# One queue of side units for VectorE through the first mixer, and a tile of their own for the new keys and values

## The chip, the cores and the metric

The kernel runs on one core of a Trainium2 chip. The metric is the time of one execution on the device in microseconds (us), lower is better. Of several runs the median is given. A separate execution is taken by the hardware profiler; its page and its trace are what is read here. TensorE is called PE in the profile, VectorE DVE, ScalarE ACT, GpSimd POOL, SyncE SP; PEld is TensorE's weight load. The program has some 47,500 instructions and is one straight line without loops on the device.

## The reference, cut to what matters

The kernel computes one inference step of a small diffusion backbone with two layers, for 128 context tokens and 128 latent tokens side by side (256 columns in the kernel). D_MODEL is 2048, everything is 32-bit floating point.

```python
for l in range(DEPTH):                                  # DEPTH = 2
    mod = jax.nn.silu(cond) @ w_ada[l] + b_ada[l]       # cond: 2 vectors, w_ada[l]: 2048 x 12288
    sh1, sc1, gt1, sh2, sc2, gt2 = jnp.split(mod[:, None, :], 6, axis=-1)
    h = rmsnorm(x, g_norm_mix[l]) * (1 + sc1) + sh1
    m = mixer_ab(h, ...) if l % 2 == 0 else mixer_c(h, ...)
    x = x + gt1 * m
    h = rmsnorm(x, g_norm_ffn[l]) * (1 + sc2) + sh2
    x = x + gt2 * conv_ffn(h, ...)

def mixer_ab(h, ...):                                   # the first mixer
    proj = h @ w_in                                     # query latent, key/value latent, rope key, qb, kb, vb
    q_lat, ckv, k_rope = ...
    kb = rmsnorm(kb, g_kn); vb = ...                    # 2 heads of new keys and values
    qa = rmsnorm(q_lat, g_q) @ w_q_up                   # 8 heads
    kv = concatenate([cached ckv, rmsnorm(ckv, g_kv)]) @ w_kv_up
    out_a = softmax_attention(qa, keys of kv and k_rope, values of kv)
    out_b = softmax_attention(qb, concatenate([cached k, kb]), concatenate([cached v, vb]))
    return concatenate([out_a, out_b]) @ w_out, (ckv, k_rope, kb, vb)
```

The new ckv, k_rope, kb and vb of the context tokens are outputs too, so the kernel stores them from the tiles in which they are made.

## The kernel before

**Large products.** Every weight matrix is read once from HBM in tiles of 1 MB (`raw`). ScalarE makes the high half of each (`wh`, L222), VectorE the low half (`wl`, L223), and TensorE multiplies three times for each block of 128 x 128: high by high, high by low, low by high (L317, L318, L321). A product of 16 blocks is 48 matmuls into one of three PSUM banks `acc`.

**The first mixer** (`mixer_ab`) runs in stages. The input projection is done in quarters of the 2048 input features, each with 23 products; the sums of the quarters are kept in `pr` (15 chunks: 6 of the query latent, 4 of the key/value latent, 1 rope key, 2 keys `kb`, 2 values `vb`) and `qb` (8 chunks). VectorE adds each product to them (L821). In the last quarter (`q == 3`) `finish` starts chains of small steps on the finished chunks: `latents` normalises the latents and stores them (L762), `keys` normalises and rotates the keys and stores them (L787), `values` transposes the values. Then come the heads: 12 products of the queries and 16 of keys and values, with two attention heads in flight between them. A query product is copied out of PSUM by ScalarE into `qn` (L903). Last is the output projection, 16 products, each followed by `residual` (L633) and a sum of squares on GpSimd (L178).

**SBUF.** The tiles of the mixer are in the pool `ab`; `ckc` and `pr` are in the pool `abp`, which is closed at the end of the input projection. The tiles of the heads (`qn`, `qr`, `p`, `kn`, `vt`, ...) are in `abh`, which is laid over the place of `abp`. A tile there waits for the last reader of the old tile that it lies over, a store to HBM among them. `pr` is one tile for this purpose.

**adaLN beside the products.** The product of the two condition vectors with w_ada (100 MB for each layer) is cut in units of 512 outputs, 48 for both layers, and mixed into the stages. There are three ways: TensorE sums rows (`sum_rows`, L445, with tiles `araw` of 1 MB, two buffers); VectorE reduces features (in the feed-forward parts); and in the first mixer a third one, the side units: 16 blocks of 256 KB for each unit (`block`, three buffers, L472), and two accumulations on VectorE for each block, one for each condition vector (`sum_block`: L456 for the first block, L459 for the others), then three small steps that reduce the two sums over partitions on TensorE, copy and transpose them. That is 16 + 3 = 19 steps for a unit. `sum_block` pins its instructions in the program's order.

**How much of it where.** After each product `pump` is called. It adds `side["rate"]` to a due count and does a step of the side units for each whole one, and the same with `RATE` for the rows. In the list of the 33 units that are summed by rows, numbers 16 to 19 are the side units: 16, 17 and 18 from the last quarter of the input projection on, with 0.6 steps a product, in the heads with 1.2, and what is left at the end of the heads is done there by `side_flush`; 19 in the output projection with 1.25. Each of the two groups has its own pair of sums `aacc` and its own blocks, in `ab` and in a pool `abo` that is laid over `ab`.

**The order on the engines** is not the program's: a scheduler gives each engine's instructions an order by its own model of the machine, except for pinned ones. Each engine then works strictly in that order, and waits at an instruction whose semaphores are not there yet. All transfers are issued by SP in one queue.

Of the kernel before, what the change touches and what calls it, by code (L numbers as in the profile page):

```python
# [17 lines left out]
P = 128  # L18
D = 2048
KD = D // P  # L20
T = 128
NT = 2 * T
# [25 lines left out]
    _AT[_name] = (_n, _w)  # L48
    _n += _w
NCONST = _n  # L50
RATE = {"in0": 0.35, "in": 0.5, "in3": 0.25, "heads": 0.75, "out0": 0.6, "c": 0.65, "outc": 0.65}
FRATE = {"up": 0.7, "down": 1.42}
PEW = {"heads": 1.0, "out0": 1.0, "c": 0.5}
QUIET = [4, 3, 3]
# [15 lines left out]
ROWS = [(0, j, q) for q in range(4) for j in (1, 0)]  # L70
# [10 lines left out]
FLIMIT = {"ab": 0, "ffn0": 12, "c": 12, "ffn1": 15}  # L81
SUMMED = [22, 24, 26, 28, 31]

BESIDE = ([16, 17, 18], [19])
SIDE = {"in3": 0.6, "heads": 1.2, "out0": 1.25}
INV = {2048: 0, 768: 1, 512: 2, 128: 3, 256: 4}


# [1 line left out]
def step_kernel(ctx: ExitStack, tc: tile.TileContext, A: dict):  # L90
    nc = tc.nc
    pe, dve, act, pool, sp = nc.tensor, nc.vector, nc.scalar, nc.gpsimd, nc.sync
# [20 lines left out]
    def T_(pl, shape, tag, dt=F32, bufs=None):  # L113
        kw = {} if bufs is None else {"bufs": bufs}
        return pl.tile(shape, dt, tag=tag, name=nm(tag), **kw)
# [109 lines left out]
    fine = [False]  # L225
# [100 lines left out]
    ada = {"i": 2, "t": 0, "due": 0.0, "pew": 1.0}  # L326
# [149 lines left out]
            side["then"] = ada_finish(*u, True, side["acc"])  # L476
            side["units"].pop(0)

    def side_start(name, units, pool_, acc):
        side.update(units=[ROWS[u] for u in units], pool=pool_, acc=acc, rate=SIDE[name], due=0.0)  # L480

    def side_pump():
        side["due"] += side["rate"]
        while side["due"] >= 1.0:
# [3 lines left out]
    def side_flush():  # L488
        while side["units"] or side["then"]:
            side_step()  # L490
# [99 lines left out]
    def modulated(st, l, which, W, fixed):  # L590


        ensure(l, 3 * which + 1)
        ensure(l, 3 * which)
        while later:
            later.pop(0)()
        if which and not l:
            ada["i"] += len(BESIDE[0]) + len(BESIDE[1])
        u = ROWS[ada["i"]]
        tile_ = lambda t: T_(wpool, [P, 4, 512], "araw", bufs=2)  # L600

        def load_tile(t):
            raw = tile_(t)
            sp.dma_start(out=raw, in_=A["w_ada"][u[0], u[1], u[2], t])
            return raw

        raws = [load_tile(0), load_tile(1)]
        hx = T_(keep, [P, KD, ROW], "hx", F32R)
        r = stat_rstd(st, D, att_bank)
        sum_rows(0, raws[0], bank())  # L610
        rb = spread(diagonal(r, (0, 1)), bank=att_bank)
        sum_rows(1, raws[1])
        raws += [load_tile(2), load_tile(3)]
        modulate(hx, rb, l, which, range(KD), fixed)
        ada["i"] += 1
        rest = ada_finish(*u, False)

        def last_rows():
            sum_rows(3, raws[3])
            rest[0]()  # L620

        def turn():
            rest[1](tc.keep_in_program_order)

        ps = first_three(W, lambda k: hx[:, k, :NT], lambda k: hx[:, k, NT:2 * NT],
                         AS_MADE if fixed else IN_TURN, lambda: sum_rows(2, raws[2]), fixed)
        W.ahead(lambda i: i)
        return hx, ps, [last_rows, turn]

    def residual(ps, l, which, c, st=None):  # L630
        for g in range(2):
            s = slice(g * T, (g + 1) * T)
            dve.scalar_tensor_tensor(out=x[:, c, s], in0=ps[:, s],  # L633
                                     scalar=mod[:, l, 3 * which + 2, c, g:g + 1],
                                     in1=x[:, c, s], op0=ALU.mult, op1=ALU.add)
        if st is not None:
            stat_add(st, x[:, c], KD)
# [62 lines left out]
        split(hx[:, c, :NT], hx[:, c, NT:2 * NT], o[:, :NT])  # L700


    def mixer_ab(hx, rb0, st):
        l = 0
        with tc.tile_pool(name="ab", bufs=1) as ab:
            with tc.tile_pool(name="abp", bufs=1) as pj:
                T_(ab, [P, SHIFT // 4], "pad")
# [15 lines left out]
                qb = T_(ab, [P, 8, NT], "qb")  # L723
                rsb = T_(ab, [P, 8, 2], "rsb")
                rsm = T_(ab, [P, 2], "rsmla")
                pr = T_(pj, [P, 15, NT], "proj")
                ck, kb, vb = pr[:, 6:10], pr[:, 11:13], pr[:, 13:15]
                sq, sk = stat_init(), stat_init()

                def queries(c):  # L730
# [82 lines left out]
                def part(W, k0, n, first, rate, between=None, **kw):  # L813

                    for c in range(23):
                        ps = gemm(W.chunk(), lambda k: hx[:, k0 + k, :NT], lambda k: hx[:, k0 + k, NT:2 * NT])
                        to = pr[:, c] if c < 15 else qb[:, c - 15]
                        if first:
                            act.copy(to, ps)
                        else:  # L820
                            dve.tensor_tensor(out=to, in0=to, in1=ps, op=ALU.add)  # L821
                        if between:
                            between(c)
                        pump(rate, **kw)
# [22 lines left out]
                for q in range(1, 4):  # L847
                    ensure(0, 1, [q])
                    ensure(0, 0, [q])
                    pinned[0] = q == 3  # L850
                    if q == 3:
                        caches()
                        acc = T_(ab, [P, 2, 512], "aacc")
                        side_start("in3", BESIDE[0], ab, [acc[:, 0], acc[:, 1]])
                    modulate(hx, rb0, 0, 0, range(4 * q, 4 * q + 4))
                    if q < 3:
                        part(W, 4 * q, 4, False, RATE["in"], until=2 * (q + 2))
                    else:
                        part(W, 4 * q, 4, False, RATE["in3"], finish)

            with tc.tile_pool(name="abh", bufs=1) as hp:
# [70 lines left out]

                    start(values_and_head(h, vt, qn[h], qr, kn))
                flush()
                side_flush()

        ensure(l, 2)
        ada["pew"] = PEW["out0"]
        W = Weights(A["w_out_ab"], KD, 1)
        oh, ol = (lambda k: o[:, k, :NT]), (lambda k: o[:, k, NT:2 * NT])  # L940
        with tc.tile_pool(name="abo", bufs=1) as abo:
            acc = T_(abo, [P, 2, 512], "aacc")
            side_start("out0", BESIDE[1], abo, [acc[:, 0], acc[:, 1]])
            for c in range(KD):
                fine[0] = c >= KD - QUIET[1]
                residual(gemm(W.chunk(), oh, ol, first=8), l, 0, c, st)
                pump(RATE["out0"] if c < KD - QUIET[1] else 0)
            side_flush()


    def mixer_c(cp, hx, W, ready, todo, st):
# [184 lines left out]
    with banks("pab") as ppool["ada"]:  # L1136
        ppool["att"] = ppool["ada"]
        for c in range(0, KD, 4):
            sp.dma_start(out=x[:, c:c + 4], in_=A["xT"][:, c:c + 4])
        first = {1: load_half(1, 0, "araw"), 0: load_half(0, 0, "raw")}  # L1140
        half_unit(1, 0, first[1], tc.keep_in_program_order)
        st = stat_init()
        for c in range(KD):
            stat_add(st, x[:, c], KD, dve)
        rb0 = norm_scale(st)
        half_unit(0, 0, first[0], tc.keep_in_program_order)
        hx = T_(keep, [P, KD, ROW], "hx", F32R)
        st = stat_init()
        mixer_ab(hx, rb0, st)
        W = Weights(A["w_up"][0], KD, 1)  # L1150
        hx, ready, todo = modulated(st, 0, 1, W, False)
    stage[0] = "ffn0"
    st = stat_init()
# [160 lines left out]
```

## Time and profile before

| | us |
|---|---|
| median of 3 runs | 2374.95 |
| lowest and highest run | 2369.23, 2376.01 |
| profiled execution | 2372.41 |
| its span, first to last instruction | 2370.6 |
| TensorE busy in the span | 2312.9 |
| VectorE busy | 1857.6 |
| ScalarE busy | 1165.7 |
| GpSimd busy | 179.7 |

The profiled execution is 1.8 us longer than its span, which is what lies around the instructions. The mean granted clock of TensorE is 0.993. The first mixer lies between about 27 and 460 us of the span: its last quarter of the input projection ends near 213 us, the heads near 363 us, and the output projection near 456 us. In the rows of waits the form is: engine, tile and line that waited, what it waited for, us in total, times, longest. In the rows of groups it is: line, engine, operation, tiles and shapes, count, then busy us, mean ns of one, and idle time of the engine just before with what ended it. In the rows of a timeline it is: start, length, engine, line, operation, tiles, count, and in brackets the idle time before. A busy TensorE is not TensorE at its peak, since matmuls are pipelined: neighbouring matmuls start about 0.11 us apart and are listed with 0.28 us each.

### The profile page before, as it was taken

The numbers are of one execution on the slowest core, as the hardware profiler recorded it, in microseconds if no ns is written. First come the engines' busy times: TensorE is split into PE (matmuls) and PEld (weight loads), VectorE is DVE, ScalarE is ACT, GpSimd is POOL, SyncE is SP. The second block draws the span as 40 slices with busy tenths as digits, with TensorE's granted clock in tenths as the row PEclk, the third lists the DMA queues.
The fourth block names the chain that finished last, engine by engine and source line by source line (L and its number), as shares of the span: only waits on it lengthen the run. The fifth ranks groups of instructions, "written<-read, shape, count | busy, mean of one in ns | idle before, by whom it ended". The sixth has DMA issues, their size and how long they took to land. (4 is left out here: it accounts for less than half of the span.)

```text
span 2370.6 us, 47563 instructions
## 1 busy us (share of the span) xinstructions
PE 2312.9 (98%) x19624; PEld 2189.4 (92%) x19624; DVE 1857.6 (78%) x2886; ACT 1165.7 (49%) x1857; POOL 179.7 (8%) x210
## 2 busy tenths in 40 slices
PE   6999999999999999999999999999999999999997
PEld 4688878899999999999989999998999999999997
DVE  3569868879999999999879887888899755666654
ACT  4345544465554355554465444446555434555543
POOL 0002211200000000001220100112000000000011
PEclk9999999999999999999999999999999999999999
DMA  9988777867777877777766787777677555555553
GB/s 370 365 306 300 291 292 263 325 223 257 267 267 275 308 265 259 263 259 274 284 232 243 286 292 278 280 292 273 246 260 259 208 196 196 194 193 191 192 194 123
DMA packets 99608, 612.95 MB, mean 259 GB/s; under 512 B 10752, under 2 KB 18624, under 8 KB 29632
## 3 DMA queue, kind: packets, MB, share of 16 engines
q1 hardware_dynamic: 99392, 609.92, 70.4%
q8 instruction: 154, 2.52, 0.4%
q14 instruction: 62, 0.51, 0.1%
HBM read 605.12 MB, written 4.75 MB: 257 GB/s over the span
## 5 line engine op out<-in xcount | busy, mean ns | idle before, releaser
L222 ACT CAST wh<-raw 128x1024 fp32r<-128x1024 f32 (+1 forms) x822 | 795.6, 979 | 914.8 <-PE acc L318 745.1
L223 DVE TENSOR_TENSOR wl<-raw,wh 128x1024 fp32r<-128x1024 f32 (+1 forms) x822 | 922.0, 1138 | 312.8 <-ACT wh L222 305.9
L317 PE MATMUL acc<-hx,wh 128*128 128x256 f32 x4064 | 1131.6, 279 | 4.1 <-ACT hx L583 3.0
L321 PE MATMUL acc<-hx,wl 128*128 128x256 f32 x4064 | 1125.5, 278 | 2.5 <-DVE wl L223 2.2
L318 PE MATMUL acc<-hx,wh 128*128 128x256 f32 x4064 | 1127.0, 278 | 0.0
L317 PEld LDWEIGHTS acc<-hx,wh 128*128 128x128 f32 x4064 | 763.6, 188 | 29.8 <-issue 14.5
L321 PEld LDWEIGHTS acc<-hx,wl 128*128 128x128 f32 x4064 | 762.4, 188 | 10.9 <-issue 3.8
L318 PEld LDWEIGHTS acc<-hx,wh 128*128 128x128 f32 x4064 | 764.3, 188 | 6.7 <-issue 5.4
L318 PE MATMUL acc<-g,wh 128*128 128x256 f32 x1408 | 388.3, 276 | 0.0
L321 PE MATMUL acc<-g,wl 128*128 128x256 f32 x1408 | 388.0, 276 | 0.0
L317 PE MATMUL acc<-g,wh 128*128 128x256 f32 x1408 | 387.8, 276 | 0.0
L430 DVE CUSTOM_DVE_ANT_0 junk<-araw,condb 128x2048 f32<-128x2048 f32 x120 | 274.6, 2288 | 0.0
L318 PEld LDWEIGHTS acc<-g,wh 128*128 128x128 f32 x1408 | 264.3, 188 | 0.0
L321 PEld LDWEIGHTS acc<-g,wl 128*128 128x128 f32 x1408 | 264.2, 188 | 0.0
L317 PEld LDWEIGHTS acc<-g,wh 128*128 128x128 f32 x1408 | 264.1, 188 | 0.0
L178 POOL TENSOR_TENSOR sqacc<-sqacc,sq 128x256 f32<-128x256 f32 x62 | 82.8, 1335 | 1520.2 <-issue 1215.8
L459 DVE SCALAR_TENSOR_TENSOR aacc<-araw,condw,aacc 128x512 f32<-128x512 f32 x150 | 111.0, 765 | 0.2
L1086 ACT ACTIVATE cv<-acc,convw 128x256 f32<-128x256 f32 x176 | 98.2, 558 | 5.3 <-PE acc L305 5.3
L459 DVE SCALAR_TENSOR_TENSOR aacc<-block,condw,aacc 128x512 f32<-128x512 f32 x120 | 90.0, 780 | 6.1 <-DMA block<-w_ada 6.0
L633 DVE SCALAR_TENSOR_TENSOR x<-acc,mod,x 128x128 f32<-128x128 f32 x192 | 57.8, 342 | 39.7 <-PE acc L321 37.4
L1089 DVE SCALAR_TENSOR_TENSOR cv<-acc,convw,cv 128x254 f32<-128x254 f32 x176 | 83.4, 474 | 5.2 <-ACT cv L1086 5.1
L1092 DVE SCALAR_TENSOR_TENSOR cv<-acc,convw,cv 128x254 f32<-128x254 f32 x176 | 84.2, 479 | 3.6
(240 smaller groups left out, 1976.5 us busy)
## 6 DMA issues: line engine op xcount, KB each, us to landing
raw<-w_up SPq DMA_DIRECT2D x176, 1024.0 KB, 4.8
araw<-w_ada SPq DMA_DIRECT2D x162, 1024.0 KB, 6.2
raw<-w_down SPq DMA_DIRECT2D x88, 1024.0 KB, 4.8
raw<-w_in_c SPq DMA_DIRECT2D x48, 1024.0 KB, 5.4
raw<-w_in_ab SPq DMA_DIRECT2D x19, 1024.0 KB, 5.7
block<-w_ada SPq DMA_DIRECT2D x64, 256.0 KB, 6.1
raw<-w_out_ab SPq DMA_DIRECT2D x16, 1024.0 KB, 7.6
raw<-w_out_c SPq DMA_DIRECT2D x16, 1024.0 KB, 6.1
```

The lines of the kernel that those rows point to most:

```text
L178: eng.tensor_tensor(out=st["acc"], in0=st["acc"], in1=sq, op=ALU.add)
L222: pin(act.copy(out_hi, src))
L223: pin(dve.tensor_tensor(out=out_lo, in0=src, in1=out_hi.bitcast(F32), op=ALU.subtract))
L317: fixed(pe.matmul(ps[:, :n], wh, xh(k), start=(i == 0), stop=False))
L318: fixed(pe.matmul(ps[:, :n], wh, xl(k), start=False, stop=False))
L321: fixed(pe.matmul(ps[:, :n], wl, xh(k), start=False, stop=(i == last)))
L430: tc.keep_in_program_order(dve.tensor_tensor_reduce(out=T_(feat["pool"], [P, D], "junk"), in1=feat["row"][:, c], in0=feat["raw"].rearrange ...
L459: i = dve.scalar_tensor_tensor(out=acc[c], in0=block, scalar=condw[:, k, c:c + 1], in1=acc[c], op0=ALU.mult, op1=ALU.add)
L633: dve.scalar_tensor_tensor(out=x[:, c, s], in0=ps[:, s], scalar=mod[:, l, 3 * which + 2, c, g:g + 1], in1=x[:, c, s], op0=ALU.mult, op1=AL ...
L1086: pin(act.activation(y, ps, AF.Identity, scale=cw[:, 1, m:m + 1], bias=cw[:, 3, m:m + 1]))
L1089: pin(dve.scalar_tensor_tensor(out=y3[:, :, 1:], in0=p3[:, :, :T - 1], scalar=cw[:, 0, m:m + 1], in1=y3[:, :, 1:], op0=ALU.mult, op1=ALU.add))
L1092: pin(dve.scalar_tensor_tensor(out=y3[:, :, :T - 1], in0=p3[:, :, 1:], scalar=cw[:, 2, m:m + 1], in1=y3[:, :, :T - 1], op0=ALU.mult, op1=A ...
```

## The change

The side units become one list that is set up once, with one pair of sums and one set of block buffers, in a pool `beside` that is opened around the whole mixer. Their step rate is 0 until the last quarter of the input projection, then 0.7 there, 1.3 in the heads and 2.0 in the output projection. Nothing is flushed between the heads and the output projection; what is left is done after the last product. The rate of the rows in the output projection goes from 0.6 to 0.55. The keys and values leave `pr` for a tile `kvb` in `ab`, so `pr` has 11 chunks. In SBUF `beside` (10 KB for a partition) stands ahead of `ab`, so the tiles of `ab` move up by that much. Each engine has the same instructions as before, in another order between the last quarter of the input projection and the start of the feed-forward part.

```diff
-RATE = {"in0": 0.35, "in": 0.5, "in3": 0.25, "heads": 0.75, "out0": 0.6, "c": 0.65, "outc": 0.65}
+RATE = {"in0": 0.35, "in": 0.5, "in3": 0.25, "heads": 0.75, "out0": 0.55, "c": 0.65, "outc": 0.65}
...
-BESIDE = ([16, 17, 18], [19])
-SIDE = {"in3": 0.6, "heads": 1.2, "out0": 1.25}
+BESIDE = [16, 17, 18, 19]
+SIDE = {"in3": 0.7, "heads": 1.3, "out0": 2.0}
...
-    def side_start(name, units, pool_, acc):
-        side.update(units=[ROWS[u] for u in units], pool=pool_, acc=acc, rate=SIDE[name], due=0.0)
...
-    def mixer_ab(hx, rb0, st):
+    def mixer_ab(hx, rb0, st, beside):
         l = 0
+        acc = T_(beside, [P, 2, 512], "aacc")
+        side.update(units=[ROWS[u] for u in BESIDE], pool=beside, acc=[acc[:, 0], acc[:, 1]])
...
-                pr = T_(pj, [P, 15, NT], "proj")
-                ck, kb, vb = pr[:, 6:10], pr[:, 11:13], pr[:, 13:15]
+                pr = T_(pj, [P, 11, NT], "proj")
+                kvb = T_(ab, [P, 4, NT], "kvb")
+                ck, kb, vb = pr[:, 6:10], kvb[:, 0:2], kvb[:, 2:4]
...
-                        to = pr[:, c] if c < 15 else qb[:, c - 15]
+                        to = pr[:, c] if c < 11 else kvb[:, c - 11] if c < 15 else qb[:, c - 15]
...
                     if q == 3:
                         caches()
-                        acc = T_(ab, [P, 2, 512], "aacc")
-                        side_start("in3", BESIDE[0], ab, [acc[:, 0], acc[:, 1]])
+                        side["rate"] = SIDE["in3"]
...
                 flush()
-                side_flush()
...
-        with tc.tile_pool(name="abo", bufs=1) as abo:
-            acc = T_(abo, [P, 2, 512], "aacc")
-            side_start("out0", BESIDE[1], abo, [acc[:, 0], acc[:, 1]])
-            for c in range(KD):
-                fine[0] = c >= KD - QUIET[1]
-                residual(gemm(W.chunk(), oh, ol, first=8), l, 0, c, st)
-                pump(RATE["out0"] if c < KD - QUIET[1] else 0)
-            side_flush()
+        side["rate"] = SIDE["out0"]
+        for c in range(KD):
+            fine[0] = c >= KD - QUIET[1]
+            residual(gemm(W.chunk(), oh, ol, first=8), l, 0, c, st)
+            pump(RATE["out0"] if c < KD - QUIET[1] else 0)
+        side_flush()
...
-        mixer_ab(hx, rb0, st)
+        with tc.tile_pool(name="beside", bufs=1) as beside:
+            mixer_ab(hx, rb0, st, beside)
```

More of the change, by code (lines that the diff above doesn't have):

```diff
@@ L597, in modulated @@
         if which and not l:
-            ada["i"] += len(BESIDE[0]) + len(BESIDE[1])
+            ada["i"] += len(BESIDE)
         u = ROWS[ada["i"]]
```

## The prediction

> **What bounds the kernel now.** I read the page first: the span, the busy times and the chain that ended last.
>
> ```profile
> span 2370.6 us, 47563 instructions
> PE 2312.9 (98%) x19624; PEld 2189.4 (92%) x19624; DVE 1857.6 (78%) x2886; ACT 1165.7 (49%) x1857; POOL 179.7 (8%) x210
> ```
>
> TensorE sets the end. The change adds and removes no instruction on any engine; it moves accumulations of VectorE (L459, two for each block of adaLN weights) and the transfers that feed them, and lays tiles elsewhere. So only time that TensorE loses around the moved work can change. Next came the busy times by stretch: the last quarter of the input projection, the heads, and the output projection in two parts.
>
> ```profile
> 183.00:215.00 32.00, 31.32 (x265) 29.80 (x264) 31.91 (x70) 17.76 (x39) 8.11 (x9) 1.00 0.76 260
> 215.00:363.00 148.00, 139.65 (x955) 107.21 (x954) 110.24 (x271) 71.32 (x172) 24.98 (x47) 0.98 0.81 300
> 363.00:402.00 39.00, 38.72 (x323) 35.45 (x321) 30.41 (x47) 18.15 (x27) 7.17 (x7) 1.00 0.74 257
> 402.00:455.00 53.00, 52.14 (x449) 48.03 (x447) 49.12 (x80) 22.97 (x35) 11.17 (x8) 1.00 0.87 317
> ```
>
> After the length come PE, PEld, DVE, ACT and POOL, then clock, DMA share, GB/s. TensorE is idle 8.35 us in the heads and under a microsecond elsewhere. VectorE is full in the first stretch (31.91 of 32), at 74% in the heads, at 93% in the last. The waits of TensorE, in the order first stretch, heads (four rows), first and second part of the output projection:
>
> ```profile
> PE att L792 <- DVE proj L821: 0.6, 2, 0.3
> ...
> PE ada L445 <- DMA araw<-w_ada: 3.8, 2, 3.6
> PE acc L317 <- ACT qn L903: 3.6, 1, 3.6
> PE att L682 <- DVE qb L651: 0.3, 1, 0.3
> PE ada L445 <- DVE mod L402: 0.3, 1, 0.3
> ...
> PE acc L321 <- DVE wl L223: 0.3, 1, 0.3
> ...
> PE ada L445 <- DMA araw<-w_ada: 0.9, 1, 0.9
> ```
>
> Two waits of 3.6 us explain most of the idle time in the heads: one for ScalarE's copy of a query, one for a tile of adaLN rows. All waits together are under 10 us, 0.4% of the span; a measurement of this kernel can tell about 0.3%, 7.1 us, from no change.
>
> **A: the copy of the queries.** Its cause is in ScalarE's and the DMA queue's rows.
>
> ```profile
> ACT qn L903 <- DMA o_gqa_k<-proj: 5.8, 1, 5.8
> ...
> 210.40 0.59 SPq L762 DMA_DIRECT2D o_ckv<-proj  x1
> ...
> 223.92 0.56 SPq L787 DMA_DIRECT2D o_gqa_k<-proj  x1
> ...
> o_ckv<-proj SPq DMA_DIRECT2D x1, 256.0 KB, 3.2
> ...
> o_gqa_k<-proj SPq DMA_DIRECT2D x1, 128.0 KB, 7.8
> ...
> 212.69 0.28 PE L317 MATMUL acc<-ql,wh 128*128 128x256 f32 x1
> 212.80 0.28 PE L318 MATMUL acc<-ql,wh 128*128 128x256 f32 x1
> ...
> 231.84 0.65 ACT L903 COPY qn<-acc 128x256 f32<-128x256 f32 x2 [5.75 <-DMA o_gqa_k<-proj]
> ```
>
> The first qn tile lies where the old projection tile lay, so it waits for that tile's last reader: the store of the new keys, issued at 223.92 and landed 7.8 us later. Two copies stand still, their sums keep their PSUM banks, and TensorE stops. With keys and values in kvb the last reader is the store of the latents: 210.40 + 3.2 = 213.6. The first query product starts at 212.69 and takes 18 matmuls, 0.11 us from start to start, to 214.7. So the wait goes: **-3.6 us**. What is late next is the key chain itself, which the first scores need. Ends: -3.6, or nothing if another hold comes at the same place.
>
> **B: the tiles of adaLN rows in the heads.**
>
> ```profile
> 342.15 0.37 SPq L508 DMA_DIRECT2D araw<-w_ada  x1
> 343.38 0.33 SPq L472 DMA_DIRECT2D block<-w_ada  x1
> ...
> 348.61 1.33 PE L445 MATMUL ada<-araw,condw 128*32 128x512 f32 x8 [3.56 <-DMA araw<-w_ada]
> ```
>
> The tile was issued at 342.15, when its buffer came free, and came just before 348.61, with blocks on both sides of it in SP's one queue. A block there waits until an accumulation frees one of three buffers, and holds up what stands behind it. The rate of rows in the heads is unchanged and more blocks than before stand there (D), so the chance of such a meeting does not fall; only its place moves. Ends: -3.8 (none meets) and +3.8 (one more of the same). I take half of the wait away, **-1.9 us**, since this one hung on an order that is drawn anew.
>
> **C, D: VectorE up to the last head.** The queue needs 4 x (16 + 3) = 76 steps. Before, 23 x 0.6 + 28 x 1.2 = 47.4 of the first three units' 57 steps are pumped by the end of the heads, the rest is flushed; now 23 x 0.7 + 28 x 1.3 = 52.5. In the built programs' order on VectorE 18 accumulations instead of 14 stand ahead of the last sum of the input projection, and 92 instead of 82 ahead of the last softmax. The old flush is no burst: just 3 accumulations stand between the last softmax and the first residual, the rest among the residuals.
>
> ```profile
> L459 DVE SCALAR_TENSOR_TENSOR aacc<-block,condw,aacc 128x512 f32<-128x512 f32 x63 | 44.8, 745 | 4.4 <-DMA block<-w_ada 4.3
> ...
> L459 DVE SCALAR_TENSOR_TENSOR aacc<-block,condw,aacc 128x512 f32<-128x512 f32 x30 | 24.2, 839 | 0.7 <-DMA block<-w_ada 0.7
> ```
>
> (Heads, then the output projection's second part.) C: 4 x 0.745 = 3.0 us more work on a full engine. Queued behind it are the sums out of PSUM, and TensorE waits for those banks. Ends 0 and +3.0; the row nearest is TensorE's 0.6 us of waits for VectorE there, so **+0.5**. D: 10 x 0.745 = 7.4 us more, against 148 - 110.24 = 37.8 us of idle time. Queued behind an accumulation are maxima and scalings of the softmaxes, ropes, and row sums; behind those, transposes on TensorE, which is in order and has only 0.3 us waits for them now. Ends 0 (all in idle time) and +7.4 (each one ahead of something awaited). An accumulation is not split, so it meets an awaited step at random; I take the middle, **+3.5**.
>
> **E: the output projection.** 36 accumulations instead of 43 remain, but they come twice per step at 2.0 steps a chunk, and end after 23.5 / 2.0 = 12 of 16 chunks.
>
> ```profile
> L223 DVE TENSOR_TENSOR wl<-raw,wh 128x1024 fp32r<-128x1024 f32 (+1 forms) x822 | 922.0, 1138 | 312.8 <-ACT wh L222 305.9
> ...
> L633 DVE SCALAR_TENSOR_TENSOR x<-acc,mod,x 128x128 f32<-128x128 f32 x17 | 5.1, 339 | 0.0
> ...
> L459 DVE SCALAR_TENSOR_TENSOR aacc<-block,condw,aacc x120: 735/744/1240, 186.8 to 452.5; 128x512 f32<-128x512 f32 x120
> ...
> L178 POOL TENSOR_TENSOR sqacc<-sqacc,sq x14: 1076/1186/1803, 379.6 to 456.1; 128x256 f32<-128x256 f32 x14
> ...
> L178 POOL TENSOR_TENSOR sqacc<-sqacc,sq x62: 730/1158/2215, 179.4 to 2350.4; 128x256 f32<-128x256 f32 x62
> ```
>
> A chunk lasts (456.1 - 379.6) / 13 = 5.88 us. VectorE needs 2 x 1.138 + 2 x 0.339 + 4 x 0.745 = 5.93 us in it, or 6.31 with the 0.839 of the last stretch. Over 12 chunks it falls 0.6 to 5.2 us behind; queued behind the accumulations are the residuals, which free TensorE's banks, and the low halves wl, which it multiplies by. Transfers: 1 MB of weights, 0.55 of rows, 0.5 of blocks, 2.05 MB in 5.88 us or about 350 GB/s, where 317 took a share of 0.87: near full, so the 0.9 us wait for rows stays. Taken **+2.5**, near the middle of 0.6 and 5.2; below nothing it can't go by more than the 0.3 + 0.9 us of waits there.
>
> The 0.839 comes from POOL: an accumulation beside a sum of squares lasts up to 1240 ns instead of 744, and the sums up to 1803 instead of 730. The Trainium skill (SBUF — State Buffer, Who interferes with whom) says that a VectorE instruction with two SBUF inputs and a GpSimd one that reads SBUF shut each other out for a whole instruction. The trace agrees, and the rule speaks against this change: with an accumulation always in the queue each of 12 sums would block one, an estimated 12 x 0.5 = 6.0 us instead of the 30 x (839 - 745) = 2.8 us that the rows show, and the total would be 3.2 us higher.
>
> **Rest.** The first tiles of the mixer move up in SBUF. Matmuls that read other addresses show what that can do:
>
> ```profile
> L317 PE MATMUL acc<-hx,wh x4064: 276/276/470, 27.7 to 2236.4; 128*128 128x256 f32 x194
> ...
> L317 PE MATMUL acc<-ql,wh x72: 276/280/468, 212.7 to 313.3; 128*128 128x256 f32 x72
> ```
>
> 4 ns on 3 x (72 + 64) matmuls is 1.6 us at most, either sign; taken as nothing. Unit 19 ends some four chunks earlier; nobody waits for it at the stage's end, so nothing.
>
> **Sum.** -3.6 - 1.9 + 0.5 + 3.5 + 2.5 = **+1.0 us**. On the profiled execution's own time that makes 2372.41 + 1.0 = 2373.4; that run lies 2.5 us under the median of 2374.95, for which I forecast **2376 us**. With all low ends (-3.6, -3.8, 0, 0, -1.2) it is -8.6, with all high ends (0, +3.8, 3.0, 7.4, 5.2) +19.4.
>
> **Rivals.** First, the waits go and idle time hides the rest: -3.6 - 3.8 - 0.9 = -8.3, **2366.6 us**. For it: VectorE idles 37.8 us in the heads. Against: the wait for rows comes from the transfers, which stay as dense.
>
> Second, slower: VectorE becomes the bound. Accumulations stand ahead of sums, residuals and softmaxes and TensorE pays for all of them: 3.0 + 7.4 + 5.2 - 3.6 = +12.0, **2387 us**. It decides in the output projection once an accumulation takes over (5.88 - 2.276 - 0.678) / 4 = 0.73 us. Both rows of accumulations exceed that, by 15 and 109 ns, which speaks for it; against it speaks that the stretch at 93% held 32 of them (30, and two that begin a pair) in 53 / 5.88 = 9 chunks, 3.6 in each, and cost TensorE no wait for VectorE.
>
> Third, the change does not do what it says: the first query copy meets the store of the latents or the key chain instead, and A is nothing: 1.0 + 3.6 = +4.6, **2379.6 us**, still within 0.3%.
>
> **How the numbers follow.** Forecast 0.46, third rival 0.06, both within 0.3%: 0.52. First rival 0.15, second 0.33, since more terms of the sum point up than down and VectorE is near full at both ends of the change. The range goes from the first rival's 2367 to just short of the second's, 2386, leaving out about half of each tail, under 2 in 10. The forecast's own range is the 0.3% on either side, 2368 to 2382.
>
> **What would show it.** Right: no wait of qn for o_gqa_k, TensorE's L317 without the 3.6 us; new waits of TensorE on VectorE in the heads (L672, L445, L879) and on wl or the residuals in the output projection, of 0.5 to 2 us each; accumulations past 1.2 us beside POOL; unit 19 done near chunk 12. Wrong: idle time in the heads falling under 2 us with no new wait (first rival), or VectorE at 97% in the output projection with chunks over 6 us (second).

## The result, and the profile after

| | before | changed |
|---|---|---|
| median of 20 runs, us | 2373.72 | 2377.63 |
| lowest and highest run | 2369.23, 2378.79 | 2373.28, 2381.82 |
| profiled execution, us | 2372.41 | 2377.45 |
| its span | 2370.6 | 2375.7 |

The ratio of the runs is 1.0018, 95% interval 1.0011 to 1.0025: slower by 2.6 to 5.9 us, still within the 0.3% that the prediction called no change. Its sum was +1.0 us, which lies below that interval; the two profiled executions differ by 5.0.

Where the time went is read first from the starts of four steps: first query product, first residual, first sum over the squares of the first mixer, first product of the second half of the feed-forward part. The rows give shortest, median and longest duration in ns, then first and last start. Before (the first of these steps, 212.7, is in the prediction):

```profile
L633 DVE SCALAR_TENSOR_TENSOR x<-acc,mod,x x192: 332/341/354, 376.7 to 2356.9; 128x128 f32<-128x128 f32 x192
L202 PE MATMUL att<-cst,sqacc x4: 169/250/250, 460.9 to 462.7; 128*128 128x1 f32 x4
L317 PE MATMUL acc<-g,wh x1408: 276/276/276, 714.6 to 2356.1; 128*128 128x256 f32 x176
```

Changed:

```profile
L317 PE MATMUL acc<-ql,wh x72: 276/276/471, 214.3 to 315.5; 128*128 128x256 f32 x72
...
L630 DVE SCALAR_TENSOR_TENSOR x<-acc,mod,x x192: 335/343/354, 379.5 to 2362.4; 128x128 f32<-128x128 f32 x192
...
L202 PE MATMUL att<-cst,sqacc x4: 168/250/250, 467.3 to 469.3; 128*128 128x1 f32 x4
...
L317 PE MATMUL acc<-g,wh x1408: 276/276/276, 719.4 to 2361.6; 128*128 128x256 f32 x176
```

The heads, here up to the first residual, went from 376.7 - 212.7 = 164.0 to 165.2 us, the output projection from 84.2 to 87.8, the stretch to the second products from 253.7 to 252.1. The 1.6 us up to the first query are taken as scatter: over all runs below that step starts anywhere from 211.5 to 216.6, and the kernel before and a run that differs from it in the heads alone (half of the accumulations, below) are 2.4 us apart there, 212.7 and 215.1. The stretch after the mixer scatters too, 252 to 254, with one exception told below (the spread version). So the change is read from two stages: heads +1.2, output projection +3.6. TensorE's waits in the changed kernel, last quarter, heads, start of the output projection:

```profile
PE att L792 <- DVE kvb L821: 0.6, 2, 0.3
PE acc L317 <- DVE proj L821: 0.2, 1, 0.2
...
PE ada L445 <- DVE mod L402: 3.0, 2, 2.7
PE att L669 <- DVE p L687: 1.6, 2, 0.9
PE misc L878 <- DVE rec L686: 1.2, 1, 1.2
PE ada L445 <- DMA araw<-w_ada: 1.0, 1, 1.0
PE ada L393 <- ACT am L386: 0.7, 1, 0.7
PE att L669 <- ACT vm L928: 0.7, 1, 0.7
PE att L694 <- ACT pT L671: 0.6, 1, 0.6
PE acc L317 <- ACT vt L920: 0.2, 1, 0.2
...
PE acc L317 <- ACT wh L222: 1.9, 2, 1.4
PE acc L321 <- DVE wl L223: 0.8, 1, 0.8
```

The wait for qn is gone and the one for araw fell from 3.8 to 1.0, but seven rows for VectorE and ScalarE, absent or 0.3 us before, stand in their place: the heads' rows add up to 9.0 us, against 8.0 before. One of them in the timeline (VectorE's and SyncE's rows, then TensorE's):

```profile
286.00 2.08 DVE L459 SCALAR_TENSOR_TENSOR aacc<-block,condw,aacc 128x512 f32<-128x512 f32 x3 [1.85 <-DMA block<-w_ada]
287.44 1.75 SPq L472 DMA_DIRECT2D block<-w_ada  x2
288.00 0.18 DVE L402 TENSOR_REDUCE mod<-ada 128x8 f32<-128x32 f32 x1
...
288.23 1.93 PE L445 MATMUL ada<-araw,condw 128*32 128x512 f32 x8 [2.69 <-DVE mod L402]
```

VectorE idles 1.85 us at an accumulation whose block has not come, then does three, and only then the small reduction for which TensorE has stood still. The idle time of VectorE at such places in the heads went from 4.3 us, 5 times, to

```profile
DVE aacc L459 <- DMA block<-w_ada: 8.9, 9, 2.7
```

In the output projection the waits lie at its start, 380 to 384 us, and there alone:

```profile
380.52 0.38 PE L317 MATMUL acc<-hx,wh 128*128 128x256 f32 x1 [0.55 <-ACT wh L222]
382.42 0.39 PE L317 MATMUL acc<-hx,wh 128*128 128x256 f32 x1 [1.39 <-ACT wh L222]
383.70 0.58 PE L321 MATMUL acc<-hx,wl 128*128 128x256 f32 x1 [0.78 <-DVE wl L223]
```

In the kernel before TensorE did two groups of row sums at this place; they need no `wh`:

```profile
376.17 1.07 PE L445 MATMUL ada<-araw,condw 128*32 128x512 f32 x8
377.60 1.07 PE L445 MATMUL ada<-araw,condw 128*32 128x512 f32 x8
```

In the built programs they stand 25 and 27 matmuls of the products after the last head before, 57 and 77 after it in the changed kernel. That their place is what matters is seen by comparing kernels, since no run moves the row sums alone: in all 14 profiled kernels of this document the waits for `wh` are at the stage's start where the first row sum stands 57 or more matmuls behind the last head, and absent where it stands at 25 to 32.

Both losses are larger than the waits themselves. Behind the longer waits TensorE's granted clock, third number from the end of these rows, is 0.50 for 3.4 us at a time, which costs 1.7 us of its work. The kernel before has two such stretches in the heads, each behind one of the two waits of 3.6 us, and none in the output projection:

```profile
233.20:236.60 3.40, 3.40 (x13) 3.40 (x12) 2.79 (x10) 3.39 (x7) 0.89 (x2) 0.50 1.00 410
349.30:352.70 3.40, 3.40 (x16) 2.55 (x13) 1.74 (x4) 1.06 (x2) 0.00 (x0) 0.50 1.04 418
```

The changed kernel has two on end in the heads, behind the wait of 2.7 us for mod, and one behind the hole:

```profile
288.10:294.80 6.70, 5.85 (x26) 2.54 (x26) 6.06 (x15) 1.34 (x3) 0.30 (x1) 0.50 0.79 272
383.60:386.90 3.30, 3.20 (x15) 3.20 (x16) 3.30 (x4) 0.00 (x0) 1.69 (x2) 0.50 0.70 238
```

With them the stages nearly add up: in the heads 1.0 us more of waits and the same 3.4 us of clock, for +1.2; in the output projection 2.7 instead of 1.2 us of waits and 1.7 instead of nothing of clock, for +3.6. The last section has this for more runs.

VectorE, meanwhile, is not the bound of the output projection. In its second part (length, PE, PEld, DVE, ACT, POOL, clock, DMA share, GB/s) it is busy for 44.82 us, where it was 49.12:

```profile
402.00:455.00 53.00, 53.00 (x455) 48.41 (x454) 44.82 (x69) 22.16 (x32) 17.47 (x9) 1.00 0.92 345
```

### The profile page after: what moved, and what is told of

The parts are those of the page before. It is cut to its first block, busy times and chain, and to the rows that moved or that the text cites. A ratio compares the mean times of both kernels' runs of the same rounds, so it can differ in the third digit from the quotient of the medians.

```text
span 2375.7 us, 47554 instructions
## 1 busy us (share of the span) xinstructions
PE 2314.4 (97%) x19624; PEld 2188.7 (92%) x19624; DVE 1858.4 (78%) x2886; ACT 1165.8 (49%) x1857; POOL 180.6 (8%) x210
## 5 line engine op out<-in xcount | busy, mean ns | idle before, releaser
L178 POOL TENSOR_TENSOR sqacc<-sqacc,sq 128x256 f32<-128x256 f32 x62 | 88.5, 1428 | 1511.5 <-issue 1210.8
```

The source lines that it names most:

```text
L178: eng.tensor_tensor(out=st["acc"], in0=st["acc"], in1=sq, op=ALU.add)
```

## Experiments on the tile of the keys and values

**Kernel before with kvb alone.**

```diff
-                pr = T_(pj, [P, 15, NT], "proj")
-                ck, kb, vb = pr[:, 6:10], pr[:, 11:13], pr[:, 13:15]
+                pr = T_(pj, [P, 11, NT], "proj")
+                kvb = T_(ab, [P, 4, NT], "kvb")
+                ck, kb, vb = pr[:, 6:10], kvb[:, 0:2], kvb[:, 2:4]
```

> The kernel before with one part of the change alone: keys and values in a tile kvb of their own, the two groups of side units and all rates as they were. Theory (term A of the prediction): the 3.6 us wait of TensorE for the query copy goes and nothing takes its place, 2373.7 - 3.6 = 2370 us, and no wait of qn for a store of more than 0.3 us is left. Rival: ScalarE or VectorE only hid behind that wait, and the next ones in their queues stop TensorE instead; the row of qn goes, and the time stays at 2373 to 2374 us.

Measured, here and below as the ratio to the kernel before and its 95% interval: 1.0008 (0.9999 to 1.0017), so -0.2 to +4.0 us. The wait for qn is gone and nothing is won. TensorE's waits in the heads:

```profile
PE att L672 <- DVE p L690: 5.8, 5, 2.2
PE misc L379 <- DVE aacc L459: 2.1, 1, 2.1
PE ada L445 <- DMA araw<-w_ada: 1.3, 1, 1.3
```

The rival holds: TensorE now stands 5.8 us for softmaxes that VectorE has yet to scale. The scheduler also gave the heads another order, so "the same program without one wait" is not what runs. (The profiled execution is the slowest of the 11 runs, 2.8 us above their median.)

**Changed kernel without kvb** (the lines above reversed).

> The changed kernel with keys and values back in proj, queue and rates as changed. Prediction's term A taken alone: the wait of the query copy for the store of the new keys is back, +3.6 us, 2381 us. Rival, from the run of kvb alone (its 3.6 us came back as 7.9 us of waits for VectorE): the heads are bound by what VectorE gets through, a wait of TensorE early in them only gives VectorE time; the copy's wait is there with 3 us or more, the later waits for VectorE shrink by as much, and the time stays within 1.5 us of 2377.6.

Measured: 1.0040 (1.0028 to 1.0052), against 1.0018 for the changed kernel: about 5 us worse, the prediction's term A and more, and not within 1.5 us of it, as the rival had it. But the waits are not simply 3.6 us of qn:

```profile
PE ada L445 <- DMA araw<-w_ada: 5.6, 2, 3.3
PE att L679 <- DVE qb L648: 2.6, 1, 2.6
PE acc L317 <- ACT qn L901: 2.6, 2, 2.2
```

So kvb is worth nothing in the old schedule and 5 us in the new one. VectorE's queue alone doesn't explain that: 92 accumulations stand ahead of the last softmax in the new schedule and 82 in the old one, and yet the tile pays there. The largest row here is the one for araw, 5.6 us against 1.0 with kvb, which is drawn anew with each order, so how much of the 5 us is kvb's stays open. Whether the queue can take the gain in the old schedule is tried in the next pair.

**Half of the accumulations in the heads, without and with kvb.** In the kernel before, and in the kernel with kvb alone, each block in the heads after the first of a unit is added to one of the two sums only.

```diff
-        for c in range(2):
+        for c in range(n):              # n = 1 in the heads, else 2
```

> The kernel before, where in the heads each block after the first of a unit is accumulated for one condition vector only (the other sum is left out there): 56 accumulations instead of 82 stand ahead of the last softmax. It is the base of the next run. Theory: the query copy still waits for the store, so TensorE's 3.6 us stay, and the rest of its waits, for rows mostly, stays too: 2370 to 2372. Rival: the heads are bound by VectorE's accumulations already in the kernel before; 2366 or less.

> The run before this one with keys and values in kvb: the part of term A again, now with VectorE relieved of 26 accumulations. Theory: term A came to nothing with kvb alone because VectorE's accumulations stood ahead of softmax scalings for which TensorE then waited 5.8 us; with half of them gone the 3.6 us come out, 3 to 4 us less than the run beside it. Rival 1: the new order of the heads, not VectorE's load, is what takes the gain; 0 to 1 us less than the run beside it, with waits of TensorE for p of 3 us or more still there. Rival 2: the copy's wait was hidden in part by other late work; then 1 to 2 us less.

Measured: without kvb 0.9991 (0.9981 to 1.0001), with kvb 0.9966 (0.9955 to 0.9977). The difference is 0.25%, 5.9 us, give or take some 3.5 us: term A comes out. Without kvb, then with it, the largest rows of TensorE's waits in the heads:

```profile
PE acc L317 <- ACT qn L903: 4.0, 1, 4.0
PE ada L445 <- DMA araw<-w_ada: 2.2, 1, 2.2
```

```profile
PE ada L445 <- DMA araw<-w_ada: 1.2, 1, 1.2
PE att L672 <- DVE p L690: 0.2, 1, 0.2
```

The wait for p, 5.8 us with all accumulations, is 0.2 with half. The order is drawn anew here too, so its share can't be kept apart from the load's; but with the load gone, the freed wait pays. That it can pay more than its 3.6 us fits the clock: the profile without kvb has five stretches at half clock in the heads, 8.5 us, the one with kvb none. (The former is the slowest of its 12 runs, 5.9 us above their median, so this is more than the usual difference.) Halving alone, with the qn wait kept, gains no more than 0.2%. That fits the reading that the wait for the store gives VectorE time to catch up and so hides its queue.

## Experiments on the rates

**The old rates in one queue.**

```diff
-SIDE = {"in3": 0.7, "heads": 1.3, "out0": 2.0}
+SIDE = {"in3": 0.6, "heads": 1.2, "out0": 1.8}
-"out0": 0.55    (rows)
+"out0": 0.6
```

> The changed kernel with the rates of before, 0.6 in the last quarter, 1.2 in the heads, rows 0.6 in the output projection, and 1.8 side steps a chunk there: one queue and kvb stay, 82 accumulations instead of 92 stand ahead of the last softmax, 14 instead of 18 ahead of the last input sum. Theory: what the change loses comes with the rates. The heads lose as much as with kvb alone (TensorE's waits 10 to 11 us, 161.3 us from first query product to last head), and at the start of the output projection the two row sums stand after 25 matmuls (27 in the kernel before) instead of 57 and cover the wait for wh: 1.9 + 0.8 us of waits gone. 2374 to 2375 us against 2373.7 of before. Rival: one queue with no flush is itself the loss, by its blocks in SP's queue and the sums beside GpSimd; 2377 us as in the changed kernel, with the wait for wh still there.

Measured: 1.0002 (0.9994 to 1.0011). The rates are what costs: about 0.16%, 3.8 us. The heads are as with kvb alone (waits for p 6.0, for the sums 2.3; 165.1 us long, in the changed kernel 165.2). The gain lies in the output projection, 82.7 us instead of 87.8: the 2.7 us of the hole and the 1.7 us of clock behind it are gone. Its start has no wait, and the two row sums are there again:

```profile
380.02 1.07 PE L445 MATMUL ada<-araw,condw 128*32 128x512 f32 x8
381.44 1.06 PE L445 MATMUL ada<-araw,condw 128*32 128x512 f32 x8
```

**Changed kernel with the old rate of rows.** Only `"out0": 0.55` becomes 0.6.

> The changed kernel with the rate of rows in the output projection back from 0.55 to 0.6, nothing else. The two row sums at the start of that stage still stand after 57 and 72 matmuls (25 and 27 before; 57 and 77 in the changed kernel), so on the theory that their place is what covers the wait for wh, that wait stays with 1.9 us and the time at 2377 to 2378. Rival: the lower rate of rows is what opened the hole; the wait goes and the time falls by 2 to 3 us.

Measured: 1.0031 (1.0019 to 1.0042), no better than the changed kernel. The hole stays with the row sums' late place, in the same two rows as in the changed kernel: 1.9 us for wh and 0.8 for wl. So it is not the rate of the rows but the side steps that made the scheduler put them later; it plans with its own model of VectorE's load. This kernel has the changed kernel's order in the heads, and yet they took 162.7 us instead of 165.2: a single profiled execution places a stage's length only to about 2.5 us. Here the trace says what they are made of: 1.1 us less of waits (7.9 instead of 9.0) and one stretch at half clock instead of two, 1.7 us.

## Experiments on the heads of the changed kernel

**A fourth buffer for the blocks**: `bufs=3` becomes `bufs=4`.

> The changed kernel with four buffers for the blocks of side weights instead of three, nothing else. Theory: TensorE's 8 us of waits for VectorE and ScalarE in the heads come from accumulations that stand at the head of VectorE's queue and wait for their block (8.9 us in the heads, 4.3 before); with a block more on the way this wait falls under 5 us, and the time by 2 to 4 us, to 2374 to 2376. Rival 1: it is the accumulations' own time, ten more of 0.75 us in front of softmaxes and row sums; then 2377 to 2378 as it was, with the wait for blocks gone or not. Rival 2: SP's one queue is the limit; a fourth block asked for earlier stands in front of the row tiles, TensorE's wait for araw grows by 1 to 3 us, 2378 to 2381.

**One sum instead of two in the heads**: the edit with `n` above, in the changed kernel.

> The changed kernel, where in the heads each block after the first of a unit is accumulated for one of the two condition vectors only; the other sum is left out there, the transfers stay. It halves VectorE's accumulations in the heads, about 34 of 67 or 25 us less. Rival 1 (their own time): the waits for VectorE in the heads fall under 3 us, and the time by 5 us or more, to 2372 or less. Theory (the wait for the block): the accumulations that are left wait for their blocks as long as now, 9 us or more, since the blocks don't come sooner; the loss in the heads falls by less than half, 2374 to 2376.

**No transfers of blocks in the heads.**

```diff
-        block = T_(side["pool"], [P, 512], "block", bufs=3)
-        sp.dma_start(out=block, in_=...)
+        if side["rate"] == SIDE["heads"]:
+            block = side["held"]          # the last block fetched
+        else: ...                         # as before, and kept in side["held"]
```

> The changed kernel, where in the heads no block is fetched: the accumulations all run, on the last block that came before the heads, so the values of those sums are not the right ones and about 9 MB of 2 KB rows aren't transferred. Theory (the wait for the block): VectorE's 8.9 us of waits for blocks are gone, and with them most of TensorE's 8 us, and the wait for araw too: 5 to 7 us less, 2371 to 2373. Rival 1 (the accumulations' own time): VectorE has the same work, TensorE's waits for it stay, 2376 to 2377.

| | ratio to before | interval |
|---|---|---|
| changed | 1.0018 | 1.0011 to 1.0025 |
| fourth buffer | 1.0016 | 1.0008 to 1.0025 |
| one sum | 0.9995 | 0.9987 to 1.0004 |
| no transfers | 1.0012 | 1.0002 to 1.0023 |

My theory from the timeline, that late blocks are what holds VectorE up, falls as the main cause. With four buffers VectorE's wait for blocks went from 8.9 us to

```profile
DVE aacc L459 <- DMA block<-w_ada: 2.1, 2, 1.1
```

and the time stayed. Rival 2 has a part in that: TensorE's waits for VectorE fell from 5.8 us to 3.8, and its wait for araw rose from 1.0 to 2.9. Without any transfers the ratio is 0.06% lower, which its interval doesn't tell from nothing. The halved sums left VectorE's wait for blocks as it was and still gained 0.23%, 5.5 us (by all runs; the profiled execution of that run is its fastest):

```profile
DVE aacc L459 <- DMA block<-w_ada: 8.8, 8, 2.4
```

What is left is the accumulations' own time in VectorE's queue (rival 1), with the reservation that this order is drawn anew too. 64 instead of 92 of them stand ahead of the last softmax, so on average one costs 5.5 / 28 = 0.2 us of its 0.75.

## Experiments for a better version

**Fewer in the heads**: 0.7, 1.0 and 2.0 side steps, rows 0.6.

> The changed kernel with 1.0 side steps a product in the heads instead of 1.3 and rows at 0.6 in the output projection: 76 accumulations instead of 92 ahead of the last softmax, the rest in the output projection at the same 2.0, ending just with it; its first row sums stand after 27 and 29 matmuls. Theory (the heads lose by the accumulations' own time, and by the blocks they wait for): 16 accumulations or 12 us of VectorE fewer take 3 us or more off the waits in the heads, and the hole of 2.7 us at the output projection's start is covered: 2370 to 2373. Rival (VectorE becomes the bound in the output projection): 16 accumulations more there, two in all 16 chunks, with sums beside GpSimd of up to 1.2 us; waits for wl or the residuals of 3 us or more appear there, 2376 to 2380.

Measured: 1.0020 (1.0001 to 1.0039). Heads 162.9 us and no hole, as the theory had it, but the side units end with the stage, and TensorE waits for a late sum of squares; the rival's waits for wl and the residuals did not come. One of the 11 runs took 2401.28 us, the others 2371.99 to 2377.13; without that one the ratio is 1.0009, so the version loses less than the 1.0020 says, and wins nothing either.

```profile
PE att L202 <- POOL sqacc L178: 4.4, 1, 4.4
```

**Spread**: 0.6, 1.1 and 2.2, rows 0.6.

> The changed kernel with 0.6, 1.1 and 2.2 side steps in the three stages and rows at 0.6 in the output projection: 14 accumulations ahead of the last input sum as before, 76 ahead of the last softmax (82 before, 92 changed), the rest over before the 15th chunk, row sums at the start of the output projection after 25 and 28 matmuls. Theory (the changed kernel loses by the hole at the output projection's start and by accumulations in the heads): no wait for wh there, TensorE's waits for VectorE in the heads 1 to 3 us below those of the run with the old rates (6.0 for p and 2.3 for the sums), no wait for the last square at the stage's end (4.4 us in the run with 1.0 in the heads): 2369 to 2372 us. Rival (VectorE becomes the bound in the output projection): waits for wl and the residuals there of 3 us or more, 2374 to 2378.

Measured: 1.0082 (1.0049 to 1.0114), which neither expected. Its 12 runs fall in two groups: six from 2373.67 to 2380.37, six from 2402.70 to 2408.53. The profiled execution, 2402.72, belongs to the second group, and its excess lies where the kernel was not touched. From 500 to 1150 us, in the feed-forward part, this run and the run with the old rates:

```profile
500.00:1150.00 650.00, 650.00 (x5522) 650.00 (x5522) 576.74 (x721) 312.74 (x410) 7.62 (x5) 1.00 0.70 257
```

```profile
500.00:1150.00 650.00, 650.00 (x5738) 650.00 (x5737) 598.51 (x746) 325.11 (x421) 16.70 (x8) 1.00 0.74 268
```

TensorE is listed as busy throughout and its clock as 1.00 in both, but it does 4% fewer matmuls in this run; no wait of TensorE is listed. The one long run of the version before, 2401.28 us, may be of the same kind; it was not profiled. The other six runs, at 1.0025 of the kernel before, still lie above the run with the old rates, so even without this the version is no gain: heads 165.2 us, waits for p of 6.5.

**The softmax scaled by ScalarE**, on the run with the old rates.

```diff
-        dve.tensor_scalar(out=p[:, :T], in0=p[:, :T], scalar1=rec[:, 0:1], scalar2=None, op0=ALU.mult)
-        dve.tensor_scalar(out=p[:, T:], in0=p[:, T:], scalar1=rec[:, 1:2], scalar2=None, op0=ALU.mult)
+        act.activation(p[:, :T], p[:, :T], AF.Identity, scale=rec[:, 0:1])
+        act.activation(p[:, T:], p[:, T:], AF.Identity, scale=rec[:, 1:2])
```

> The run with the old rates (one queue, kvb, 0.6 / 1.2 / 1.8), where the two scalings of each softmax by its reciprocals are done by ScalarE instead of VectorE: 32 scalings or 10 us less for VectorE in the heads, 1 us more for ScalarE in each of 16 softmaxes, which idles 77 of 148 us there. Theory (VectorE's queue takes term A's 3.6 us in the heads): TensorE's 6.0 us of waits for p fall to 2 or less and no other wait takes their place, 3 to 4 us less than the 2372.6 of that run, 2368 to 2370 and under the kernel before. Rival 1: the reciprocal itself stands behind the accumulations; the wait only moves from p to the reciprocal, ScalarE waits for it with the casts wh and the copies behind it, 2372 to 2376. Rival 2: the scalings on ScalarE stand ahead of wh and of the copies out of PSUM; TensorE's waits for ScalarE rise by 3 us or more, 2375 to 2380.

Measured: 0.9983 (0.9974 to 0.9992), median 2367.18 us against 2371.77 of before beside it: 1.9 to 6.2 us faster than the kernel before, and so faster than both. The wait for p fell from 6.0 to 1.8 us, the one for the sums from 2.3 to 0.6, and TensorE's other waits for ScalarE stayed at 1.2 us together (1.3 with the old rates alone):

```profile
PE ada L445 <- DMA araw<-w_ada: 2.0, 2, 1.4
PE att L669 <- ACT p L687: 1.8, 3, 1.0
PE misc L379 <- DVE aacc L459: 0.6, 1, 0.6
```

ScalarE waits 2.7 us for reciprocals in all, so rival 1 is there, but small. The heads took 160.9 instead of 165.1 us, without a stretch at half clock where the run with the old rates has one.

## Why the prediction was right or wrong

The forecast, no change that can be told, a little to the slow side, came out; its terms did not all. In the heads they came to -3.6 - 1.9 + 3.5 = -2.0 us where +1.2 was measured, in the output projection to +2.5 where it was +3.6. The band of 7.1 us either way was wide enough for this, so the number is in part luck. One price is missing from all of them: a long wait was counted with its length alone, and the clock of 0.98 in the row of the heads was left aside. Each of the two waits of 3.6 us had 1.7 us of lost clock behind it, so by these lengths about 5.3 us hung on each.

**A, the query copy: the mechanism right, the gain wrong.** The wait went as described. That -3.6 us would come out was the step that failed: "what is late next" was named as the key chain, and it was VectorE, with softmax scalings behind accumulations. The kvb tile alone brought nothing in the old schedule; with half of the accumulations gone, 5.9 us. A wait of 3.6 us on TensorE was also 3.6 us in which VectorE worked off its queue. In the changed kernel itself, taking kvb away cost 5 us, which this account doesn't cover.

**B, the row tiles: near, by luck of the draw.** -1.9 was taken, and the row fell by 2.8. In the other runs it was between 0.2 and 5.6, which bears out that the meeting is drawn anew with each order.

**C, the last quarter: right.** 0.2 us of waits for sums where +0.5 was taken; VectorE is as full as before.

**D, the heads: size too high, and put on the wrong base.** Ten more accumulations were to cost 3.5 us, 0.35 each. The halved sums give 0.2 each on average, and between the old rates and the changed ones the heads differ by less than one execution's scatter. The waits for VectorE that appear are there with 82 accumulations as well (7.9 us with kvb alone), so they go with A's wait, which had hidden them, and not with the ten more.

**E, the output projection: near in size, wrong in mechanism.** +2.5 was worked out from VectorE falling behind by up to 0.43 us a chunk; the stage did grow by 3.6 us, but VectorE has spare time there and holds nothing up after 384 us. The loss is the hole of 2.7 us at the start, which the two row sums used to cover, and the 1.7 us of clock behind it. Their new place could be seen in the built program; the prediction counted the accumulations in that order and not the row sums, and took the rows' part as transfers only.

**The lock of VectorE and GpSimd: seen, and without effect on the end.** By the rule of the Trainium skill (SBUF — State Buffer, Who interferes with whom) the prediction had made an estimate of 6.0 us. The trace agrees with the rule in kind: in the changed kernel the 32 accumulations that overlap a GpSimd instruction take 881 ns on average, the 88 others 746. In the output projection the 34 accumulations take 842 ns each, so 34 x (842 - 745) = 3.3 us over their time in the heads; before it was 832. GpSimd paid more, its sums of squares took up to 3601 ns where the longest was 1803:

```profile
L178 POOL TENSOR_TENSOR sqacc<-sqacc,sq x14: 938/1492/3601, 383.1 to 463.4; 128x256 f32<-128x256 f32 x14
```

Neither engine is awaited there, so nothing follows for the time.

**Rest.** The accumulations end at 438 instead of 452 us, as said, and nobody waits for it. The 4 ns of matmul duration were put down to addresses; the runs do not bear that out, see below.

**The rivals.** VectorE did not become the bound of the output projection (second), and the waits did not go with the rest hidden (first). The third, that A gives nothing, was right for kvb by itself, but by VectorE and not by the hold that it named.

What stays open: how much of the 5.9 us of the pair with halved sums comes from the new order and not from VectorE's load, since every edit redraws the order; why kvb is worth 5 us in the new schedule; and why the spread version took this longer pace in half of its runs.

## What to carry to other kernels

When a wait on the bounding engine is to be removed, look at what the other in-order engines did in that time: if one of them has a queue, the wait may have been paying for it, and the gain comes only with that queue made shorter. Price the wait with the clock behind it: here a long one cost half as much again as its length. Moving side work on one engine makes a scheduler move other things as well; compare the place of every filler in the two built orders, not just the work that was meant to move. A few microseconds of one stage in one profiled execution can be scatter: a second kernel with the same order there shows how much, and the stage's waits and granted clock show of what.

## What the runs showed of the hardware that was not expected

**A long wait of TensorE is followed by time at half clock.** The granted clock in these traces is 1.00 or 0.50, and 0.50 comes in stretches of 3.4 us, at times two or three on end. In the heads and the output projection every wait of 2.6 us or more, in any run, has one that begins within 3 us of the wait's end; so does the hole, with its waits of about 0.55, 1.4 and 0.8 us within 4 us, in all five kernels that have it. Of the waits between 1 and 2.4 us some have one and some don't. In the four runs without such a stretch in the heads no wait there is over 1.8 us. Matmuls that start 0.12 us apart start 0.21 apart in it. That the wait brings it on is read from this order of events; no run tests it by itself. The length of the heads, less TensorE's waits and less 1.7 us for each stretch, is nearly the same in all (us):

| heads of | length | waits | stretches | what is left |
|---|---|---|---|---|
| kernel before | 164.0 | 8.0 | 2 | 152.6 |
| changed | 165.2 | 9.0 | 2 | 152.8 |
| kvb alone | 165.2 | 10.5 | 1 | 153.0 |
| old rates in one queue | 165.1 | 11.0 | 1 | 152.4 |
| halved, without kvb | 166.3 | 6.9 | 5 | 150.9 |
| halved, with kvb | 154.4 | 1.4 | 0 | 153.0 |
| softmax scaled by ScalarE | 160.9 | 5.8 | 0 | 155.1 |

**TensorE has two steady paces for the same matmuls at the same granted clock.** In the profiled execution of the spread version nearly all of the 5,515 spacings of the 128 x 256 matmuls between 500 and 1150 us were 116 to 120 ns (mean 117.8); in the run with the old rates one or two of 5,730, with a mean of 113.3. The rows of one line over that stretch, spread version and old rates:

```profile
L317 PE MATMUL acc<-hx,wh 128*128 128x256 f32 x1344 | 377.6, 281 | 0.0
```

```profile
L317 PE MATMUL acc<-hx,wh 128*128 128x256 f32 x1341 | 370.1, 276 | 0.0
```

It set in at 503 us, without a wait, where four small matmuls stand between those of the product, and held until the stream was next broken, at 1224 us:

```profile
502.99 0.60 PE L393 MATMUL misc<-cst,am 128*128 128x128 f32 x4
```

The same four matmuls stand at this place in the other 13 profiled executions, and the pace behind them is 113 ns there. In the 650 us shown, 5,520 matmuls at 4.42 ns make 24 us, and the whole stretch from break to break, 6,116 of them, 27 us: the 26 us between the medians of the two groups of runs. All kernels show shorter stretches of both paces in the mixers (about half of such spacings at the longer one in the heads before, about a quarter in the changed kernel), worth a microsecond at most there. Nearly every stretch of ten or more of these matmuls with nothing between them keeps one pace, so it changes where the stream is broken. The product around 503 us reads the same tiles ahead of the break and behind it, which speaks against their address as the cause. What decides the pace behind a break was not found.
